# A hybrid decoder trunk on one core: recurrent projections first, attention columns later, and a second set of tiles for the recurrent group

## The chip, the cores and the metric

The kernel runs on one core of a Trainium2 chip. The core has five engines with their own instruction queues: TensorE (PE, matmuls, with its weight loads shown apart as PEld), VectorE (DVE), ScalarE (ACT), GpSimd (POOL) and SyncE (SP), which issues the DMAs here. The metric is device time of one execution in microseconds. Single executions are profiled; there is no number for a cost that is not read from such a profile.

## The reference, cut to what matters

Two layers, 256 tokens, width 2048, float32. Each layer has a mixer and a channel part:

```python
for l in range(2):
    mod = silu(c) @ w_ada[l] + b_ada[l]             # 6 vectors of 2048 ("ada")
    u = x * (1 + sc_m) + sh_m
    proj = u @ w_in[l]                              # 4896 columns
    q, k, v = proj[..., :1024], proj[..., 1024:1280], proj[..., 1280:1536]
    y_attn = sliding_window_attention(q, k, v, ...) # 16 heads of 64, 4 kv heads, window 128
    y_rwkv = rwkv7_group(proj[..., 1536:], ...)     # 16 heads of 64
    mix = concat([y_attn, y_rwkv]) @ w_out[l]
    x = layer_norm(alpha * x + gt_m * mix)
    u = x * (1 + sc_f) + sh_f
    gate, up = split(u @ w_gate_up[l])
    x = layer_norm(alpha * x + gt_f * ((silu(gate) * up) @ w_down[l]))
```

`rwkv7_group` shifts its columns by a token, splits them into r, k, v and three low-rank inputs, and runs a recurrence per head, one token after the other:

```python
S = S * w_t + (S @ a_t) b_t^T + v_t k_t^T           # S is 64 x 64 per head
o_t = S @ r_t
```

with a decay `w` and a gate `a` from low-rank products, then a group norm, a bonus term and a gate.

## The kernel before

**Precision.** Weights come in as float32 tiles of 512 KB (`raw`, L373), are cast on ACT to a rounded `hi` (L380) and the rest `lo = raw - hi` is made on DVE (L381, "the weight split"). Each product is then three matmuls, hi by hi, lo by hi, hi by lo: L402, L403, L405 where tokens are on the output's partitions (128x512 outputs), L414 to L416 in `tstream` where columns are (128x256 outputs). `raw` has 4 buffers, `hi` 3 and `lo` 2.

**Ada steps.** The modulation vectors are products of one row with `w_ada`: DVE sums a 512 KB tile `ast` times a scalar into `aacc` (L257), one step at a time, with two buffers. A pump in `steps()` and an `adv()` in the recurrence hand such steps out between other work; each is tied behind the latest weight split. SP issues all DMAs, weights, ada tiles and the mixer's own small ones, from one in-order queue.

**The mixer.** The recurrent part is done chunkwise: 4 chunks of 64 tokens, 8 pairs of heads in 4 groups of two pairs. For a group g the pieces are:

- D, `decays` (from L590): low-rank matmuls `zb` (L598) and `ab`, decay exponentials `e1` and `e2`, the gate `tha`, and `de`, three diagonal tiles per pair.
- R, `project` (from L576): the r and k columns by `tstream`.
- A, `prepare` (from L630): token shift, normalisation, the matrices `aa` (L684) and their masked copies `am` (L687), then `ax`, `at` (L702), `kb` (L710, the matmul with `de`) and `bnb` (L718).
- I, `invert` (from L723): the triangular inverse. The 16x16 diagonal blocks go out and in through DMA, POOL does 30 small steps (L729 to L735), DMA puts the result into `tinv` and back into `tm`, and two levels follow, each a DVE transpose `ytr` (L745), PE `m` (L749), DVE `yx` (L752), PE `m` (L756).
- C, `recur` (from L760): products with `tm`, then the chunk recurrence over ACT's state copies (L830).
- E, `close` (from L834): norm and gate.

Q0 to Q2, `project_qkv` (L869), are the attention columns in three blocks of 512, each with 96 matmuls and eight weight tiles; an ACT copy `stg` (L875) and a DMA write the block to `qkv` in HBM. X closes the pool of the recurrent tiles (`pa`) and opens that of attention (`pt`). Then a, b and c are the rotation (L884, reading `qkv` back), the weighting and the gathering for each of the four kv heads, and w and z the output projection (L995 on) over attention's and the recurrence's rows.

**What sets the order.** A string per layer, `ORDER` (L41), is the order in which the pieces are written. A scheduler then builds every engine's instruction stream ahead of the run, from that program order, the tiles' buffer counts and its own estimates; the streams are fixed and in order on each engine. A tile's buffer count says how many groups can hold it at the same time.

Of the kernel before, what the change touches and what calls it, by code (L numbers as in the profile page):

```python
# [10 lines left out]
F32 = mybir.dt.float32  # L11
# [8 lines left out]
P = 128  # L20
D = 2048
T = 256
# [16 lines left out]
DECAY = math.exp(-0.5)  # L39
NEG = -3.0e38  # L40
ORDER = (  # L41
    "D0 R0 A0 D1 I0 R1 C0 E0 Q1 A1 I1 D2 R2 A2 Q0 D3 C1 R3 E1 I2 A3 X Q2 a0 a1 b0 C2 a2 b1 c0 E2 a3 c1 I3 b2 b3 c2 c3 w0 C3 w1 w2 E3 z0 z1 z2 z3 w3",
    "D0 R0 A0 D1 R1 I0 C0 Q2 E0 A1 I1 D2 R2 A2 D3 Q1 C1 R3 E1 A3 I2 Q0 X a0 a1 b0 b1 c0 C2 I3 a2 b2 E2 a3 c1 b3 c2 c3 w0 C3 z0 w1 w2 E3 z1 z2 z3 w3",
)
PARTS = (4, 4, 2, 4, 2)
LAG = 2
# [21 lines left out]
def hybrid_trunk_kernel(  # L68
# [421 lines left out]
    def mixer(l, us, mixp, feeds):  # L490
# [7 lines left out]
        x0 = {}  # L498
        if rk:
            for i, s in ((0, 1), (0, 0), (1, 0)):  # L500
                x0[i, s] = pa.tile([P, T], F32, tag=("t_xr", "t_xk")[s], name="x0", bufs=2)
                shift_mix(l, x0[i, s], rk[i][s], 8 * s + i)
            turn[1] = 1

# [19 lines left out]
        if l > 0:  # L524
            v1t = pa.tile([P, NPAIR, 32], F32, tag="w2a2", name="v1t", bufs=1)
            dma(v1t, rwkv_v1[l - 1].rearrange("(q p) n -> p q n", p=P))
            hv = twd[64:96, :]
            b = bank()
            for p in range(NPAIR):
                PE.matmul(b[64:96, 0:T], lhsT=v1t[:, p, :], rhs=vx[:, p, :], start=(p == 0), stop=(p == NPAIR - 1))  # L530
            S.copy(hv, b[64:96, 0:T])
            for p2 in range(4):
                b = bank()
                v2t = pa.tile([P, T], F32, tag="w2a2", name="v2t", bufs=1)
                dma(v2t[64:96, :], rwkv_v2[l - 1, :, p2 * T:(p2 + 1) * T])
                for i in range(2):
                    p = 2 * p2 + i
                    PE.matmul(b[:, i * T:(i + 1) * T], lhsT=v2t[64:96, i * P:(i + 1) * P], rhs=hv, start=True, stop=True)
                for i in range(2):
                    p = 2 * p2 + i  # L540
                    gt = pa.tile([P, T], F32, tag="t_tha", name="gt", bufs=2)
                    S.activation(gt, b[:, i * T:(i + 1) * T], AF.Tanh, scale=0.5, bias=drv(l, "v0h", p))
                    vf = pa.tile([P, T], F32, tag="t_e2", name="vf", bufs=2)
                    dma(vf, vfirst[p])
                    V.tensor_sub(vf, vf, vx[:, p, :])
                    V.scalar_tensor_tensor(vf, gt, 1.0, vf, ALU.add, ALU.mult)
                    V.scalar_tensor_tensor(vx[:, p, :], vf, 0.5, vx[:, p, :], ALU.mult, ALU.add)
# [42 lines left out]
        def decays(g):  # L590
# [11 lines left out]
            for i in I2:  # L602
                s_, p = st[i], 2 * g + i
                lw = pa.tile([P, T], F32, tag="t_lw", name="lw", bufs=2)
                S.activation(lw, zb[:, i * T:(i + 1) * T], AF.Tanh, scale=0.5, bias=drv(l, "w0h", p))
                s_["tha"] = tha = pa.tile([P, T], F32, tag="t_tha", name="tha", bufs=2)
                S.activation(tha, ab[:, i * T:(i + 1) * T], AF.Tanh, scale=0.5, bias=drv(l, "a0h", p))
                V.tensor_scalar(lw, lw, -0.5 * DECAY, -0.5 * DECAY, ALU.mult, ALU.add)
                V.tensor_tensor_scan(lw, rmask, lw, 0.0, ALU.mult, ALU.add)
                s_["e1"] = e1 = pa.tile([P, NCH, CH + 1], F32, tag="e1", name="e1", bufs=2)  # L610
                V.memset(e1[:, :, 0:1], 1.0)
                S.activation(e1[:, :, 1:CH + 1], lw.rearrange("p (c s) -> p c s", s=CH), AF.Exp)
                s_["el"] = el = pb.tile([P, NCH, 1], F32, tag="el", name="el", bufs=4)
                G.tensor_copy(el, e1[:, :, CH:CH + 1])
                s_["de"] = de = pa.tile([P, NCH - 1, P], F32, tag="de", name="de", bufs=2)
                for cc in range(NCH - 1):
                    S.activation(de[:, cc, :], ident, AF.Copy, scale=e1[:, cc, CH:CH + 1])
                s_["e2"] = e2 = pa.tile([P, T], F32, tag="t_e2", name="e2", bufs=2)
                S.activation(e2, lw, AF.Exp, scale=-1.0)
            vt_ = bank("vt")  # L620
            for cc in range(NCH):
# [8 lines left out]
        def prepare(g, st, bk):  # L630

            nscr = dram.tile([4 * NCH, CH + 1, CH], F32, tag="nscr", name="nscr", bufs=3)
            for i in I2:
                s_, p = st[i], 2 * g + i
                for s, nm in ((1, "xk"), (0, "xr")):
                    if g == 0 and (i, s) in x0:
                        s_[nm] = x0[i, s]
                    else:
                        s_[nm] = pa.tile([P, T], F32, tag=f"t_{nm}", name=nm, bufs=2)
                        shift_mix(l, s_[nm], bk[i][:, s * T:(s + 1) * T], 8 * s + p)  # L640
            ssb = bank("ssb")
            for i in I2:
# [62 lines left out]
            for i in I2:  # L705
                s_ = st[i]
                bkc = s_["bkc"]
                kb = bank("kb")
                for cc in range(NCH - 1):
                    PE.matmul(kb[:, cc * P:(cc + 1) * P], lhsT=bkc[:, cc, :], rhs=s_["de"][:, cc, :], start=True, stop=True)  # L710
                s_["bkt"] = bkt = pb.tile([P, NCH - 1, P], F32, tag="bkt", name="bkt", bufs=4)
                S.copy(bkt.rearrange("p c s -> p (c s)"), kb[:, 0:(NCH - 1) * P])
            bnb = bank("bnb")
# [155 lines left out]
        def project_qkv(c0):  # L869
# [1 line left out]
            bk = acc_banks(1)  # L871
            stream(cols(w_in[l], c0, 512), 512, list(range(KT)), us, [(0, 512)], bk)
            for t in range(2):
                sg = (pt or pa).tile([P, 512], F32, tag="stg", name="stg", bufs=2)
                S.copy(sg, bk[t][0])  # L875
                dma(qkv[l, t, :, c0:c0 + 512], sg)

# [474 lines left out]
```

## Time and profile before

| | us |
|---|---|
| median of 3 runs | 2697.75 (2696.93 to 2700.12) |
| the profiled execution | 2698.87 |
| its span in the trace | 2697.1 |
| PE, DVE, ACT, POOL busy | 2507.4, 1843.0, 1189.2, 132.2 |
| prologue and the first projections of layer 0 | 0 to 178 |
| mixer, layer 0, projections; then inversion and attention | 178 to 423; 423 to 542 |
| mixer, layer 1, projections; then inversion and attention | 1518 to 1762; 1762 to 1845 |

The profiled execution's time and its span differ by 1.8 us, which lie around the first and last recorded instruction. Times in rows are from the span's start. A busy PE is not a PE at its peak; the granted clock beside it says how fast it ran.

### The profile page before, as it was taken

How to read it: one execution, taken by the hardware profiler on the slowest of the kernel's cores; microseconds unless marked ns; L12 is line 12 of the kernel's file. 1: busy time of each engine (PE TensorE's matmuls, PEld its weight loads, DVE VectorE, ACT ScalarE, POOL GpSimd, SP SyncE). 2: the span in 40 equal slices, each digit the busy share in tenths (PEclk: the TensorE clock that was granted, in tenths of full speed). 3: DMA queues.
4: the chain of work that ended last, by engine and by line, in shares of the span. 5: the costliest groups of instructions: out<-in, count | busy, mean ns of one | idle time of the engine just before them, and what ended most of it. 6: DMA issues, size and time to landing. Idle time of an engine off the chain costs nothing.

```text
span 2697.1 us, 41748 instructions
## 1 busy us (share of the span) xinstructions
PE 2507.4 (93%) x15325; PEld 2097.6 (78%) x15325; DVE 1843.0 (68%) x2469; ACT 1189.2 (44%) x2029; POOL 132.2 (5%) x355
## 2 busy tenths in 40 slices
PE   3789998797999999999999989989999999999997
PEld 3787886576878888888889877867788888888887
DVE  6867767979877777777788676565864545545456
ACT  2364452435444444444445544534444444344442
POOL 1002111000000000000000022110000000000000
PEclk9789997898999999999999999979999999999999
DMA  9968667598988888889878586424756655656654
GB/s 308 383 193 255 196 196 236 180 333 280 349 309 309 303 298 306 301 296 313 307 267 298 170 247 202 119 73 149 249 170 190 188 188 194 196 188 188 194 187 149
DMA packets 351999, 637.49 MB, mean 236 GB/s; under 512 B 75894, under 2 KB 142898, under 8 KB 350258
## 3 DMA queue, kind: packets, MB, share of 16 engines
q1 hardware_dynamic: 351794, 634.82, 71.4%
q8 instruction: 120, 1.97, 0.3%
q14 instruction: 85, 0.70, 0.1%
HBM read 622.08 MB, written 12.62 MB: 235 GB/s over the span
## 4 chain that ended last, share of the span: by engine, by line
PE 74%; DMA 12%; DVE 8%; issue 2%; POOL 2%; ACT 1%; SPq 1%; DVEq 0%; POOLq 0%; ACTq 0%
PE acc L403 19%; PE acc L405 19%; PE acc L402 19%; DMA ast<-in_w_ada_dram 7%; PE acc L416 3%; PE acc L415 3%; PE acc L414 3%; DVE lo L381 2%; DVE aacc L257 2%; DMA raw<-in_w_in_dram 1%; DMA raw<-in_w_gate_up_dram 1%; POOL tmp L733 1%; DMA raw<-in_w_out_dram 1%; PE aa L684 1%; PE mb L1225 1%
## 5 line engine op out<-in xcount | busy, mean ns | idle before, releaser
L380 ACT CAST hi<-raw 128x1024 fp32r<-128x1024 f32 (+2 forms) x728 | 758.3, 1044 | 1101.1 <-PE acc L405 811.6
L381 DVE TENSOR_TENSOR lo<-raw,hi 128x1024 fp32r<-128x1024 f32 (+2 forms) x728 | 880.6, 1212 | 519.4 <-PE acc L403 337.4
L403 PE MATMUL acc<-lo,u 128*128 128x512 f32 x1568 | 513.0, 394 | 9.2 <-DVE lo L381 9.2
L405 PE MATMUL acc<-hi,u 128*128 128x512 f32 x1568 | 506.1, 391 | 0.0
L257 DVE SCALAR_TENSOR_TENSOR aacc<-ast,cond,aacc 128x1024 f32<-128x1024 f32 x300 | 384.4, 1281 | 130.9 <-DMA ast<-in_w_ada_dram 129.6
L402 PE MATMUL acc<-hi,u 128*128 128x512 f32 x1568 | 458.0, 393 | 0.5 <-ACT u L360 0.5
L403 PEld LDWEIGHTS acc<-lo,u 128*128 128x128 f32 x1568 | 294.0, 189 | 74.2 <-DVE lo L381 13.4
L402 PEld LDWEIGHTS acc<-hi,u 128*128 128x128 f32 x1568 | 295.0, 189 | 62.2 <-ACT u L360 0.9
L405 PEld LDWEIGHTS acc<-hi,u 128*128 128x128 f32 x1568 | 295.2, 188 | 61.9 <-issue 0.7
L403 PE MATMUL acc<-lo,ht 128*128 128x512 f32 (+1 forms) x720 | 243.6, 377 | 2.7 <-DVE lo L381 2.6
L405 PE MATMUL acc<-hi,ht 128*128 128x512 f32 (+1 forms) x720 | 242.2, 375 | 0.0
L414 PE MATMUL acc<-u,hi 128*128 128x256 f32 x720 | 207.9, 295 | 13.1 <-ACT hi L380 13.1
L402 PE MATMUL acc<-hi,ht 128*128 128x512 f32 (+1 forms) x720 | 217.0, 376 | 0.0
L415 PE MATMUL acc<-u,hi 128*128 128x256 f32 x720 | 207.3, 295 | 0.0
L416 PE MATMUL acc<-u,lo 128*128 128x256 f32 x720 | 195.0, 297 | 3.5 <-DVE lo L381 3.5
L414 PEld LDWEIGHTS acc<-u,hi 128*128 128x128 f32 x720 | 144.3, 201 | 17.6 <-ACT hi L380 14.0
L403 PEld LDWEIGHTS acc<-lo,ht 128*128 128x128 f32 x720 | 135.0, 188 | 29.2 <-DVE lo L381 5.5
L405 PEld LDWEIGHTS acc<-hi,ht 128*128 128x128 f32 x720 | 135.6, 188 | 24.2
L402 PEld LDWEIGHTS acc<-hi,ht 128*128 128x128 f32 x720 | 134.8, 188 | 24.4
L415 PEld LDWEIGHTS acc<-u,hi 128*128 128x128 f32 x720 | 144.1, 200 | 3.6 <-issue 2.8
L416 PEld LDWEIGHTS acc<-u,lo 128*128 128x128 f32 x720 | 136.0, 201 | 7.7 <-DVE lo L381 5.1
L1067 POOL TENSOR_TENSOR brs<-brs,mhalf 128x1 f32<-128x1 f32 x8 | 6.5, 808 | 1705.3 <-DVE brs L1066 883.2
(349 smaller groups left out, 2887.8 us busy)
## 6 DMA issues: line engine op xcount, KB each, us to landing
ast<-in_w_ada_dram SPq DMA_DIRECT2D x368, 512.0 KB
raw<-in_w_gate_up_dram SPq DMA_DIRECT2D x704, 256.0 KB
raw<-in_w_down_dram SPq DMA_DIRECT2D x176, 512.0 KB
raw<-in_w_in_dram SPq DMA_DIRECT2D x82, 512.0 KB
raw<-in_w_out_dram SPq DMA_DIRECT2D x64, 512.0 KB
raw<-in_w_in_dram SPq DMA_DIRECT2D x120, 256.0 KB
ast<-in_w_ada_dram SPq DMA_DIRECT2D x32, 256.0 KB
lnw<-in_ln_w_dram SPq DMA_DIRECT2D x4, 1024.0 KB
```

The costliest lines, as they stand in the source:

```text
L257: ins = V.scalar_tensor_tensor(acc, t, cond[:, j:j + 1], acc, ALU.mult, ALU.add)
L380: S.copy(h, fl)
L381: ins = V.tensor_tensor(r, fl, h.bitcast(F32), ALU.subtract)
L402: PE.matmul(bt, lhsT=xh, rhs=hi[:, c0:c0 + w], start=st, stop=False)
L403: PE.matmul(bt, lhsT=xh, rhs=lo[:, c0:c0 + w], start=False, stop=False)
L405: PE.matmul(banks[t][q][:, 0:w], lhsT=xl, rhs=hi[:, c0:c0 + w], start=False, stop=sp_)
L414: PE.matmul(bt, lhsT=hi[:, c0:c0 + w], rhs=xh, start=st and opens, stop=False)
L415: PE.matmul(bt, lhsT=hi[:, c0:c0 + w], rhs=xl, start=False, stop=False)
L416: PE.matmul(bt, lhsT=lo[:, c0:c0 + w], rhs=xh, start=False, stop=sp_ and closes)
L684: PE.matmul(aas[h][:, cc * P:(cc + 1) * P], lhsT=bkc[hs, cc, :], rhs=ar[hs, cc, :], start=True, stop=True)
L733: G.tensor_tensor(tmp[:, 0:cm, 0:w], nb[:, s:s + 1, s + 1:].to_broadcast([P, cm, w]), tt[:, 0:cm, s:s + 1].to_broadcast([P, cm, w]), ALU.mult)
L1225: PE.transpose(b[:, i * T + t * P:i * T + (t + 1) * P], hh[t][:, (2 * k2 + i) * P:(2 * k2 + i + 1) * P], ident)
```

## The change

The diff. In both layers the string has the recurrent pieces first, Q1 behind A3, and Q0 and Q2 behind X; the tiles `xk`, `tha` (with `gt`), `e2` (with `vf`) and `e1` go from two to four buffers, `stg` from two to one, and the copies that make `de` move from `decays` to `prepare`.

```diff
 ORDER = (
-    "D0 R0 A0 D1 I0 R1 C0 E0 Q1 A1 I1 D2 R2 A2 Q0 D3 C1 R3 E1 I2 A3 X Q2 a0 a1 b0 C2 a2 b1 c0 E2 a3 c1 I3 b2 b3 c2 c3 w0 C3 w1 w2 E3 z0 z1 z2 z3 w3",
-    "D0 R0 A0 D1 R1 I0 C0 Q2 E0 A1 I1 D2 R2 A2 D3 Q1 C1 R3 E1 A3 I2 Q0 X a0 a1 b0 b1 c0 C2 I3 a2 b2 E2 a3 c1 b3 c2 c3 w0 C3 z0 w1 w2 E3 z1 z2 z3 w3",
+    "D0 R0 A0 D1 I0 R1 C0 A1 D2 I1 E0 R2 A2 D3 C1 I2 R3 E1 A3 Q1 C2 I3 X Q0 Q2 a0 a1 b0 E2 b1 c0 c1 a2 a3 b2 C3 b3 c2 E3 c3 w0 w1 w2 z0 z1 z2 z3 w3",
+    "D0 R0 A0 D1 R1 I0 C0 A1 D2 I1 E0 R2 A2 D3 C1 I2 R3 E1 A3 Q1 C2 I3 X Q0 Q2 a0 a1 b0 E2 b1 c0 c1 a2 a3 b2 C3 b3 c2 E3 c3 w0 w1 w2 z0 z1 z2 z3 w3",
 )
@@ mixer()
-                x0[i, s] = pa.tile([P, T], F32, tag=("t_xr", "t_xk")[s], name="x0", bufs=2)
+                x0[i, s] = pa.tile([P, T], F32, tag=("t_xr", "t_xk")[s], name="x0", bufs=(2, 4)[s])
...
-                    gt = pa.tile([P, T], F32, tag="t_tha", name="gt", bufs=2)
+                    gt = pa.tile([P, T], F32, tag="t_tha", name="gt", bufs=4)
...
-                    vf = pa.tile([P, T], F32, tag="t_e2", name="vf", bufs=2)
+                    vf = pa.tile([P, T], F32, tag="t_e2", name="vf", bufs=4)
@@ decays()
-                s_["tha"] = tha = pa.tile([P, T], F32, tag="t_tha", name="tha", bufs=2)
+                s_["tha"] = tha = pa.tile([P, T], F32, tag="t_tha", name="tha", bufs=4)
...
-                s_["e1"] = e1 = pa.tile([P, NCH, CH + 1], F32, tag="e1", name="e1", bufs=2)
+                s_["e1"] = e1 = pa.tile([P, NCH, CH + 1], F32, tag="e1", name="e1", bufs=4)
...
-                s_["de"] = de = pa.tile([P, NCH - 1, P], F32, tag="de", name="de", bufs=2)
-                for cc in range(NCH - 1):
-                    S.activation(de[:, cc, :], ident, AF.Copy, scale=e1[:, cc, CH:CH + 1])
-                s_["e2"] = e2 = pa.tile([P, T], F32, tag="t_e2", name="e2", bufs=2)
+                s_["e2"] = e2 = pa.tile([P, T], F32, tag="t_e2", name="e2", bufs=4)
@@ prepare()
-                        s_[nm] = pa.tile([P, T], F32, tag=f"t_{nm}", name=nm, bufs=2)
+                        s_[nm] = pa.tile([P, T], F32, tag=f"t_{nm}", name=nm, bufs=(2, 4)[s])
...
                 bkc = s_["bkc"]
+                de = pa.tile([P, NCH - 1, P], F32, tag="de", name="de", bufs=2)
+                for cc in range(NCH - 1):
+                    S.activation(de[:, cc, :], ident, AF.Copy, scale=s_["e1"][:, cc, CH:CH + 1])
                 kb = bank("kb")
                 for cc in range(NCH - 1):
-                    PE.matmul(kb[:, cc * P:(cc + 1) * P], lhsT=bkc[:, cc, :], rhs=s_["de"][:, cc, :], start=True, stop=True)
+                    PE.matmul(kb[:, cc * P:(cc + 1) * P], lhsT=bkc[:, cc, :], rhs=de[:, cc, :], start=True, stop=True)
@@ project_qkv()
-                sg = (pt or pa).tile([P, 512], F32, tag="stg", name="stg", bufs=2)
+                sg = (pt or pa).tile([P, 512], F32, tag="stg", name="stg", bufs=1)
```

In the streams below a row is a line, an operation, output and inputs, the output's shape and a count. Lines 617 to 704 of the changed kernel are three lower than the same code before.

PE in layer 0, from the last matmul of the attention columns (L405). Before:

```order
L405 MATMUL acc<-hi,u 128x512
L684 MATMUL aa<-ar,bkc 128x128 x8
L756 MATMUL m_4318<-tm,yx 64x64 x16
L695 MATMUL ax<-uv,am 64x64 x16
L702 MATMUL at<-ident,ar 64x128 x6
L769 MATMUL ta<-atl,tm 64x64 x11
L710 MATMUL kb<-de,bkc 128x128 x3
L769 MATMUL ta<-atl,tm 64x64
L710 MATMUL kb<-de,bkc 128x128 x3
L775 MATMUL tk<-uv,tm 64x64 x10
L718 MATMUL bnb<-xr,bones 128x256
```

Now:

```order
L405 MATMUL acc<-hi,u 128x512
L811 MATMUL ob<-state_1664,rh 64x128 x2
L814 MATMUL ob<-uv,am 64x64 x4
L749 MATMUL m_4543<-ytr,am 64x64 x16
L756 MATMUL m_4562<-tm,yx 64x64 x16
L906 MATMUL acc<-ident,qr 128x128 x6
L749 MATMUL m_4582<-ytr,am 64x64 x16
L906 MATMUL acc<-ident,qr 128x128 x4
L756 MATMUL m_4601<-tm,yx 64x64 x16
L906 MATMUL acc<-ident,qr 128x128 x2
L925 MATMUL acc<-qT 128x256 x4
```

Before, preparation of group 3 (`aa`, `ax`, `at`, `kb`, `bnb`) and the recurrence of group 2 (`ta`, `tk` with `tm` of the inversion before) stand behind the last projection matmul. Now they stand ahead of it, and what follows is the end of that recurrence (`ob`) and the inversion of group 3 (`m` with its `ytr` and `tm`), ahead of attention's transposes (L906).

DVE in layer 0, around the transpose `ytr` of the last inversion before the change:

```order
L894 TENSOR_TENSOR ra<-qk,cosk 128x640
L895 TENSOR_TENSOR rb<-qk,sink__147 128x640
L852 TENSOR_SCALAR vr<-vr 128x8
L898 TENSOR_TENSOR qr<-ra,rb 128x5x32
L899 TENSOR_TENSOR qr<-ra,rb 128x5x32
L898 TENSOR_TENSOR qr<-ra,rb 128x5x32
L899 TENSOR_TENSOR qr<-ra,rb 128x5x32
L257 SCALAR_TENSOR_TENSOR aacc<-ast,cond,aacc 128x1024
L854 TENSOR_TENSOR sq<-os__4848,vr 128x512
L257 SCALAR_TENSOR_TENSOR aacc<-ast,cond,aacc 128x1024
L745 STREAM_TRANSPOSE ytr<-tm 128x512
L894 TENSOR_TENSOR ra<-qk,cosk 128x640
```

The same transpose, that of group 3's inversion, in the changed kernel (`bv` ends group 3's preparation, L381 are weight splits, L894 is the first rotation):

```order
L720 TENSOR_TENSOR bv<-bnb,vx 128x256
L381 TENSOR_TENSOR lo<-raw,hi 128x1024
L745 STREAM_TRANSPOSE ytr<-tm 128x512
L255 TENSOR_SCALAR aacc<-ast,cond 128x1024
L257 SCALAR_TENSOR_TENSOR aacc<-ast,cond,aacc 128x1024
L381 TENSOR_TENSOR lo<-raw,hi 128x1024
L284 SCALAR_TENSOR_TENSOR mods_135<-asum,par_131 128x8
L257 SCALAR_TENSOR_TENSOR aacc<-ast,cond,aacc 128x1024
L381 TENSOR_TENSOR lo<-raw,hi 128x1024
L894 TENSOR_TENSOR ra<-qk,cosk 128x640
```

Before, the transpose stands behind the first rotation (`ra` to `qr`) and ada steps (L257), and ahead of the second rotation. Now it stands one weight split behind the preparation's `bv`, ahead of two weight splits, ada steps and the first rotation.

DVE in layer 1, at the transpose of group 2's inversion. Before:

```order
L381 TENSOR_TENSOR lo<-raw,hi 128x1024
L745 STREAM_TRANSPOSE ytr<-tm 128x512
L798 TENSOR_TENSOR mt<-mr,mt 128x256
L800 TENSOR_TENSOR rh<-mr,ar 128x192
L798 TENSOR_TENSOR mt<-mr,mt 128x256
L800 TENSOR_TENSOR rh<-mr,ar 128x192
L381 TENSOR_TENSOR lo<-raw,hi 128x1024 x4
L455 SCALAR_TENSOR_TENSOR xk<-acc,par_132,xk 128x255 x2
```

Now:

```order
L455 SCALAR_TENSOR_TENSOR xr<-acc,par_132,xr 128x255
L745 STREAM_TRANSPOSE ytr<-tm 128x512
L662 SCALAR_TENSOR_TENSOR ar<-xk,der_134,e_15817 128x4x64
L675 TENSOR_TENSOR ar<-xr,e_15817 128x4x64
L798 TENSOR_TENSOR mt<-mr,mt 128x256
L800 TENSOR_TENSOR rh<-mr,ar 128x192
L662 SCALAR_TENSOR_TENSOR ar<-xk,der_134,e_15830 128x4x64
L675 TENSOR_TENSOR ar<-xr,e_15830 128x4x64
L381 TENSOR_TENSOR lo<-raw,hi 128x1024 x7
L752 TENSOR_TENSOR yx<-m_16056,mmask 128x512
```

The transpose `ytr` and six instructions of preparation and recurrence stand ahead of seven weight splits; before, four recurrence instructions and then four splits stood behind it.

## The prediction

> **What bounds the kernel now.** I read the page first, then the stretches of the two mixers engine by engine, then single instructions at the seams. The page says where there is room:
>
> ```profile
> span 2697.1 us, 41748 instructions
> PE 2507.4 (93%) x15325; PEld 2097.6 (78%) x15325; DVE 1843.0 (68%) x2469; ACT 1189.2 (44%) x2029; POOL 132.2 (5%) x355
> PEclk9789997898999999999999999979999999999999
> ```
>
> TensorE (PE) is busy 93% of the span, and the granted clock dips in slices 6 to 8 (337 to 539 us) and 28 (1821 to 1888 us): the ends of the two mixers. The change edits only the mixers, so I cut these into stretches. Columns: window, length, busy us of PE, weight load, VectorE (DVE), ScalarE (ACT), GpSimd (POOL), granted clock, DMA share, GB/s.
>
> ```profile
> 178.00:423.00 245.00, 234.87 (x2244) 201.81 (x2243) 179.78 (x275) 124.82 (x249) 40.98 (x103) 0.96 0.72 221
> 423.00:464.00 41.00, 32.30 (x313) 24.74 (x312) 26.29 (x39) 13.07 (x41) 11.64 (x33) 0.72 0.77 216
> 464.00:542.00 78.00, 56.96 (x558) 44.38 (x557) 71.44 (x192) 31.75 (x120) 2.22 (x3) 0.78 0.61 183
> 1518.00:1762.00 244.00, 230.98 (x2195) 195.86 (x2193) 165.39 (x257) 122.03 (x257) 46.32 (x103) 0.97 0.63 190
> 1762.00:1791.00 29.00, 18.65 (x293) 14.90 (x292) 12.84 (x27) 9.88 (x24) 9.55 (x33) 0.85 0.45 108
> 1791.00:1845.00 54.00, 48.48 (x511) 36.80 (x510) 39.08 (x157) 25.69 (x98) 1.34 (x3) 0.83 0.04 11
> ```
>
> Rows one and four are the projections: PE has 10 us idle in 245 and 13 us in 244, so PE sets the pace. Behind them come *bare* stretches without projection matmuls. The second and fifth are inversions, chains over POOL, DMA and DVE. The third is attention in layer 0, with DVE busy 71.4 of 78 us: there DVE sets the pace. PE idles 8.7, 21.0, 10.4 and 5.5 us in the bare rows. The seams (columns: start, length, engine, line, operation, tiles; in brackets the idle time before and its releaser):
>
> ```profile
> 178.07 0.48 PE L598 MATMUL zb<-twd,w2a 64*128 64x256 f32 x1
> 421.62 0.39 PE L405 MATMUL acc<-hi,u 128*128 128x512 f32 x1
> 426.56 0.68 DVE L687 TENSOR_TENSOR am<-aa,amask 128x512 f32<-128x512 f32 x1
> 464.20 0.71 DVE L745 STREAM_TRANSPOSE ytr<-tm 128x512 f32<-128x512 f32 x1
> 530.61 0.50 PE L402 MATMUL acc<-hi,yl 128*128 128x512 f32 x1
> 542.42 2.35 DVE L381 TENSOR_TENSOR lo<-raw,hi 128x1024 fp32r<-128x1024 f32 x2
> 1761.50 0.40 PE L403 MATMUL acc<-lo,u 128*128 128x512 f32 x1
> 1761.73 0.40 PE L405 MATMUL acc<-hi,u 128*128 128x512 f32 x1
> 1763.25 1.29 DVE L687 TENSOR_TENSOR am<-aa,amask 128x512 f32<-128x512 f32 x2
> 1790.83 0.71 DVE L745 STREAM_TRANSPOSE ytr<-tm 128x512 f32<-128x512 f32 x1 [1.05 <-DMA tm<-tinv]
> 1845.19 0.50 PE L402 MATMUL acc<-hi,yl 128*128 128x512 f32 x1
> ```
>
> Layer 0: the last query/key/value matmul starts at 421.6, the last inversion runs from its mask (am, done at 427.2) to its transpose (ytr) at 464.2, 37.0 us, the first output-projection matmul at 530.6, and DVE is through with attention at 542.4, where the projection's third weight split starts. Layer 1: 1761.7, 1790.8, 1845.2. Starts of neighbouring matmuls lie 0.23 us apart. Behind both seams PE is saturated until the layer's end, so what the change is worth is how far 542.4 and 1845.2 move.
>
> **The double tiles and `de`.** By the order, decays D(n+1)'s first matmul (zb) stands right behind preparation A(n)'s last (bnb) before the change, and still does or is at most a few projection matmuls later. The second set of tiles therefore moves the decays hardly at all: 0. The `de` copies are the same three ACT instructions per pair, on an engine busy 125 of 245 us: 0, between -1 and +1 for both together. What acts is the new string: recurrences earlier, and A3's tail with C2 under query/key/value projections where they stood behind the last of these.
>
> **Layer 0, the projections.** The moved work costs PE time in a full stretch. A window that holds such a pair (A2's tail with C1, and decays D3), and in it the projection's matmuls alone:
>
> ```profile
> 350.00:381.00 31.00, 31.00 (x378) 27.58 (x378) 12.09 (x19) 18.10 (x46) 9.24 (x33) 1.00 0.43 109
> 350.00:381.00 31.00, 16.58 (x118) 14.57 (x118) 0.00 (x0) 0.00 (x0) 1.00 0.43 109
> ```
>
> 31.0 - 16.6 = 14.4 us, less about 2 for D3 (my estimate): the moved pair costs 12 to 13 us, 12.5 taken. The last projection matmul goes from 421.6 to 434.1, if no inversion is late. Whether one is depends on its length:
>
> ```profile
> 290.15 0.28 PE L415 MATMUL acc<-u,hi 128*128 128x256 f32 x1
> 290.27 0.28 PE L416 MATMUL acc<-u,lo 128*128 128x256 f32 x1
> 290.03 1.29 DVE L687 TENSOR_TENSOR am<-aa,amask 128x512 f32<-128x512 f32 x2 [0.65 <-PE aa L684]
> 315.88 0.70 DVE L745 STREAM_TRANSPOSE ytr<-tm 128x512 f32<-128x512 f32 x1
> 217.44 1.28 DVE L687 TENSOR_TENSOR am<-aa,amask 128x512 f32<-128x512 f32 x2
> 254.05 0.70 DVE L745 STREAM_TRANSPOSE ytr<-tm 128x512 f32<-128x512 f32 x1
> 251.34 1.28 DVE L257 SCALAR_TENSOR_TENSOR aacc<-ast,cond,aacc 128x1024 f32<-128x1024 f32 x1 [6.98 <-DMA ast<-in_w_ada_dram]
> 227.50:246.00 18.50, 18.50 (x96) 14.47 (x95) 14.12 (x17) 10.28 (x21) 15.79 (x30) 1.00 0.62 225
> 297.50:309.20 11.70, 11.70 (x108) 8.75 (x106) 4.66 (x9) 8.73 (x23) 8.98 (x32) 1.00 0.40 131
> ```
>
> From the mask's end to ytr it is 24.6 us (291.3 to 315.9) or 35.3 (218.7 to 254.1). POOL's thirty small steps take 9.0 us beside a quiet DVE (4.7 busy of 11.7) and 15.8 beside a busy one (14.1 of 18.5). The 7 us wait for `ast` sits at the end of the slow chain, since its loads stand on SyncE's queue behind the inversion's own, and ytr stands behind that step on DVE.
>
> In the new order PE has, between group 1's `aa` and its first inversion matmul, 72 receptance/key matmuls 0.12 us apart (8.6), such a pair (C0 with A1's tail, 12.5) and D2 (2): 23 us. A chain of 25 to 37 leaves PE waiting 2 to 14 us, and I take 7, the side of the quick one. The second inversion has more cover: 0 to 6, taken 2. The last projection matmul is then at 434.1 + 9 = 443 (435 to 453).
>
> Group 3's mask is some 28 us ahead of that (75 matmuls of 0.23, and 11 of the moved 12.5), at 415. With a chain of 25 to 37, taken 31 since DVE there still splits weights, ytr is at 446 instead of 464.2: **18 us won**, 439 to 452.
>
> **Layer 0, attention.** DVE's queue between ytr and the third output split now holds more, because ytr moved ahead of it: by the order 33 ada steps for 26, 188 other instructions for 166.
>
> ```profile
> 464.00:542.00 78.00, 31.98 (x26) 0.78 0.61 183
> L257 DVE SCALAR_TENSOR_TENSOR aacc<-ast,cond,aacc 128x1024 f32<-128x1024 f32 x34 | 43.7, 1285 | 15.7 <-DMA ast<-in_w_ada_dram 15.3
> L894 DVE TENSOR_TENSOR ra<-qk,cosk 128x640 f32<-128x640 f32 x4 | 3.3, 824 | 0.2 <-DMA qk<-qkv 0.2
> L895 DVE TENSOR_TENSOR rb<-qk,sink__147 128x640 f32<-128x640 f32 x4 | 3.3, 816 | 0.0
> L898 DVE TENSOR_TENSOR qr<-ra,rb 128x160 f32<-128x160 f32 x8 | 2.6, 320 | 0.1
> ```
>
> Line one is the ada part (L257) of the attention stretch, the others are groups of 423 to 540. The added work is 7 ada steps at 1.29 (9.0), two rotations at 0.82 + 0.82 + 4 x 0.32 = 2.9 (5.8), and two weight splits of 2.35 together (row at 542.42): 17.2, some 17.5 with E2's small ones. So 71.4 + 17.5 = 88.9 us of DVE work. Before, 6.6 us of 78 were waits; I take 7.5, between 0 and 15 (C2's and E2's matmuls are no longer in this stretch, but I3's now stand at its start). 446 + 96.4 = 542.4, against 542.4: **0**. By that time some ten fewer output matmuls are done, since E2's and attention's feeds for them come later: 10 x 0.23 = 2.3. **Layer 0: +3**, from -8 (439, no added wait) to +16 (452, 104 us).
>
> **Layer 1.** Its slow spot before:
>
> ```profile
> 1659.67 1.29 DVE L257 SCALAR_TENSOR_TENSOR aacc<-ast,cond,aacc 128x1024 f32<-128x1024 f32 x1 [6.92 <-DMA ast<-in_w_ada_dram]
> 1662.14 0.79 PE L403 MATMUL acc<-lo,u 128*128 128x512 f32 x1 [4.82 <-DVE lo L381]
> PE mb L277 <- DVE aacc L257: 7.1, 1, 7.1
> 1791.00:1845.00 54.00, 0.00 (x0) 0.83 0.04 11
> ```
>
> There a late ada step held a weight split and so PE, 4.8 and 7.1 us; these waits go or change place (between 0 and -12, -6 taken). New is that group 2's ytr stands on DVE ahead of seven weight splits: PE has 46 projection matmuls whose weights are split and a pair of 12.5 until it needs them, 23 us against a chain of 25 to 37: wait 2 to 14, 8 taken, and 2 for group 1. With the moved 12.5 the last matmul goes from 1761.7 to 1778 (1768 to 1788). Group 3's mask lies 16 us ahead of it (34 matmuls and 8 of the moved work), at 1762; with the 26.3 of before (1764.54 to 1790.83) ytr comes at 1788 to 1789, where it was at 1790.8. The stretch behind it took 54.4 and no ada step lies in it. C2 has left it, but attention's rotations and E2 have not, so PE's part shrinks little: between 52 (its 48.5 busy us and few waits) and 64 (the inversion stretch's 10.4 us of idle on top), and I take 58, the middle. 1789 + 58 = 1847 against 1845.2; **+3** with the single staging tile's small waits in it, from -7 (ytr at 1783 and 55 us) to +12 (1793 and 64).
>
> **Sum.** +3 and +3 on the profiled 2698.87 gives 2705; that execution is 1.1 above the median of 2697.75, so **2704**.
>
> The Trainium skill, "SBUF — State Buffer", section "Who interferes with whom", says that a DVE instruction with two SBUF inputs contends with a GpSimd instruction that reads SBUF. The rows 15.79 beside 14.12 and 8.98 beside 4.66 agree with it. By that rule alone every inversion laid under weight splits runs at the slow pace, and the sum would be 2704 + 2 x 5 = 2714, an estimate.
>
> **The rivals.** 0.2% of 2698 is 5.4 us, about what a measurement of this kernel can tell from no change.
> (a) *Forecast, slower by some us*, 0.39: PE pays 12.5 us per layer in full stretches, and what it frees is eaten by DVE's longer attention queue. For: DVE busy 71.4 of 78. Against: PE idles 21 us there. Range of its own 2699 to 2716.
> (b) *No change*, 0.25: the decays stay where they are, and what ytr wins in each layer the stretch behind it loses, to a few us: 2698. For: both sums above end within 3 us of zero. Against: they have bounds of 19 and 24 us between them, and nothing makes the two sides equal.
> (c) *Faster*, 0.30: the inversions keep the fast pace (24.6) because DVE has fewer late ada steps beside them. Then PE waits nowhere in the projections (ytr at 439 and 1783): -7 and -6 against the profiled run, 2698.9 - 13 - 1.1 = 2685, itself 2680 to 2692. For: 4.8 and 7.1 us that layer 1 loses now. Against: both slow chains lie where DVE splits weights.
> (d) *The single staging tile*, 0.06: its second copy (L875) waits on ACT for the first write, which on SyncE's queue stands behind the last inversion's `tinv` and `tm` loads. C2's state copies and a weight cast stand behind it on ACT. If the write is held for the whole POOL part (9 to 16 us), one such hold in each layer adds 5 to 8 beside what PE still has to do: 2704 + 11 = 2715. It decides once the write's issue is more than about 5 us late.
>
> The likeliest is (a), 2704. From (c)'s lower part to the upper bounds of (a) and (d), 2682 to 2724 leaves about 2 in 10 out. Slower: four fifths of (a) and (d), 0.37; same: (b) and the rest of (a), 0.33; faster: (c), 0.30.
>
> **What would show it.** Layer 0's last inversion transpose at 446 and the third output split at 542 or later, with DVE over 85 us busy between. The last projection matmuls near 443 and 1778. Waits of PE for DVE at m (L749) or at a weight split, 2 to 14 us, at the inversions of group 1 in layer 0 and group 2 in layer 1. Wrong: those waits absent and the output projection beginning before 526 or 1840, which is (c); or a gap on ACT ahead of the second staging copy over 5 us, which is (d).

## The result and the profile after

The changed kernel took 2710.22 us (median of 5 runs, 2704.71 to 2714.87) against 2697.75 (5 runs); the ratio is 1.0035, with a 95% interval of 1.0018 to 1.0052. Run once more beside the experiments it took 2708.05 (8 runs), ratio 1.0031 (1.0018 to 1.0044). It is slower by 10 to 12 us between medians; the forecast was 2704, 6 us slower.

The page of the changed kernel. The profiled execution took 2704.71 us, the quickest of its five.

```profile
span 2703.0 us, 41745 instructions
PE 2502.6 (93%) x15325; PEld 2094.4 (77%) x15325; DVE 1841.0 (68%) x2469; ACT 1188.5 (44%) x2029; POOL 133.2 (5%) x355
PEclk9899998799999999999999998979999999999999
```

All engines are busy for about the same time as before. The windows are cut at the same events as before the change (columns as in the prediction): projections, last inversion, attention, for each layer.

```profile
174.00:419.00 245.00, 228.87 (x2363) 196.09 (x2363) 181.56 (x278) 120.38 (x246) 42.53 (x103) 0.97 0.70 212
419.00:444.00 25.00, 21.54 (x147) 17.06 (x145) 10.14 (x13) 7.46 (x19) 10.86 (x30) 0.93 0.72 215
444.00:548.00 104.00, 65.86 (x609) 50.94 (x609) 88.24 (x220) 44.15 (x163) 7.32 (x6) 0.74 0.67 205
1517.00:1762.00 245.00, 233.88 (x2355) 199.43 (x2354) 166.83 (x261) 120.30 (x255) 41.78 (x107) 0.97 0.63 184
1762.00:1779.00 17.00, 12.55 (x117) 9.58 (x115) 4.75 (x6) 8.04 (x17) 8.19 (x27) 0.95 0.40 115
1779.00:1855.00 76.00, 61.59 (x547) 46.17 (x548) 47.91 (x178) 31.90 (x109) 4.46 (x6) 0.72 0.13 39
```

The seams of the changed kernel, from its timeline:

```profile
174.15 0.48 PE L598 MATMUL zb<-twd,w2a 64*128 64x256 f32 x1
443.14 0.71 DVE L745 STREAM_TRANSPOSE ytr<-tm 128x512 f32<-128x512 f32 x1 [5.07 <-DMA tm<-tinv]
443.76 0.39 PE L405 MATMUL acc<-hi,u 128*128 128x512 f32 x1
541.48 0.47 PE L402 MATMUL acc<-hi,yl 128*128 128x512 f32 x1
548.04 1.23 DVE L381 TENSOR_TENSOR lo<-raw,hi 128x1024 fp32r<-128x1024 f32 x1 [1.82 <-PE acc L403]
1517.25 0.48 PE L598 MATMUL zb<-twd,w2a 64*128 64x256 f32 x1
1772.39 0.39 PE L405 MATMUL acc<-hi,u 128*128 128x512 f32 x1
1778.81 0.71 DVE L745 STREAM_TRANSPOSE ytr<-tm 128x512 f32<-128x512 f32 x1 [4.93 <-DMA tm<-tinv]
1854.76 0.50 PE L402 MATMUL acc<-hi,yl 128*128 128x512 f32 x1
```

In layer 0 the last inversion's transpose comes 21 us earlier than before (443.1 for 464.2), the last projection matmul 22 us later, and the first output-projection matmul 11 us later (541.5 for 530.6); this execution entered the layer 3.9 us earlier, so counted from the layer's first decay matmul it is 14.8. In layer 1 the transpose comes 12 us earlier (1778.8 for 1790.8) and the first output matmul 9.6 us later (1854.8 for 1845.2). In both layers the inversion is won and the start of the output projection is lost.

What the late start is worth differs. These are windows of the output projections, of layer 0 and of layer 1, in the kernel before:

```profile
560.00:600.00 40.00, 35.24 (x148) 26.95 (x147) 29.91 (x36) 13.35 (x14) 0.00 (x0) 1.00 0.98 365
1855.00:1900.00 45.00, 43.59 (x192) 35.12 (x191) 27.12 (x38) 20.23 (x23) 0.14 (x1) 1.00 0.76 270
```

and that of layer 0 in the changed kernel:

```profile
560.00:600.00 40.00, 38.56 (x166) 30.26 (x165) 32.49 (x37) 14.75 (x15) 0.00 (x0) 1.00 0.97 371
```

In layer 0 the projection caught up: its last matmul started at 635.1 before and at 635.0 now, 3.9 us late instead of 14.8 when counted from the layer's start. From its first matmul to its last it took 104.5 us before and 93.5 now. The DMA engines are as busy in the one as in the other (0.98 and 0.97), so their share does not tell the two apart. PE's waits do (who waited for what, us in total, times, longest). Before, from 530.6 to 636, PE was idle for 9.0 us, with these among its waits:

```profile
PE acc L402 <- DVE yl L460: 2.7, 1, 2.7
PE acc L402 <- ACT yl L459: 1.4, 1, 1.4
```

Here `yl` is a row of attention or recurrence, rounded for the projection. In the changed kernel, from 541.5 to 636, PE was idle for 2.1 us, and its waits are for weights alone:

```profile
PE acc L403 <- DVE lo L381: 1.0, 4, 0.3
PE acc L402 <- ACT hi L380: 0.9, 1, 0.9
```

The other part of the 11 us is PE's own pace: in the first 29 us of the projection the granted clock was 0.94 before and 1.00 after. The later profiles agree: this projection takes 101.9 to 104.6 us with the old string in layer 0, with 7.7 to 9.5 us of idle time and `yl` among the waits, and 93.5 to 97.4 with the new string, with 2.1 to 4.1 us idle and no wait for `yl`. The new string closes the recurrence (C3, E3) ahead of the projection, which fits; which of its pieces frees the rows was not taken apart. In layer 1 PE was idle for 1.8 us of this projection before, and 3 of the 11 us were made up (95.0 and 92.2 us).

### The profile page after: what moved, and what is told of

It is laid out like the page before. It is cut to its first block, busy times and chain, and to the rows that moved or that the text cites. A ratio compares the mean times of both kernels' runs of the same rounds, so it can differ in the third digit from the quotient of the medians.

```text
span 2703.0 us, 41745 instructions
## 1 busy us (share of the span) xinstructions
PE 2502.6 (93%) x15325; PEld 2094.4 (77%) x15325; DVE 1841.0 (68%) x2469; ACT 1188.5 (44%) x2029; POOL 133.2 (5%) x355
## 4 chain that ended last, share of the span: by engine, by line
PE 60%; DMA 4%; DVE 4%; POOL 1%; ACT 1%; issue 1%; SPq 0%; DVEq 0%; POOLq 0%; ACTq 0%
PE acc L403 17%; PE acc L405 17%; PE acc L402 17%; DVE lo L381 1%; PE acc L414 1%; PE acc L415 1%; PE acc L416 1%; POOL tmp L733 1%; DMA raw<-in_w_gate_up_dram 1%; PE mb L1225 1%; DVE aacc L257 1%; DMA raw<-in_w_out_dram 1%; DMA nscr<-am 1%; POOL ttl L735 1%; DMA nb<-nscr 0%
## 5 line engine op out<-in xcount | busy, mean ns | idle before, releaser
L381 DVE TENSOR_TENSOR lo<-raw,hi 128x1024 fp32r<-128x1024 f32 (+2 forms) x728 | 879.9, 1211 | 513.7 <-PE acc L403 350.4
L405 PE MATMUL acc<-hi,u 128*128 128x512 f32 x1568 | 507.7, 392 | 0.0
L257 DVE SCALAR_TENSOR_TENSOR aacc<-ast,cond,aacc 128x1024 f32<-128x1024 f32 x300 | 383.8, 1279 | 128.2 <-DMA ast<-in_w_ada_dram 127.2
L405 PEld LDWEIGHTS acc<-hi,u 128*128 128x128 f32 x1568 | 296.0, 189 | 62.4 <-DVE u L361 0.3
L403 PE MATMUL acc<-lo,ht 128*128 128x512 f32 (+1 forms) x720 | 243.5, 377 | 2.2 <-DVE lo L381 2.2
L405 PE MATMUL acc<-hi,ht 128*128 128x512 f32 (+1 forms) x720 | 242.2, 375 | 0.0
L414 PEld LDWEIGHTS acc<-u,hi 128*128 128x128 f32 x720 | 143.5, 200 | 15.8 <-ACT hi L380 12.5
L405 PEld LDWEIGHTS acc<-hi,ht 128*128 128x128 f32 x720 | 135.6, 188 | 24.3
```

The source lines that it names most:

```text
L257: ins = V.scalar_tensor_tensor(acc, t, cond[:, j:j + 1], acc, ALU.mult, ALU.add)
L381: ins = V.tensor_tensor(r, fl, h.bitcast(F32), ALU.subtract)
L403: PE.matmul(bt, lhsT=xh, rhs=lo[:, c0:c0 + w], start=False, stop=False)
L405: PE.matmul(banks[t][q][:, 0:w], lhsT=xl, rhs=hi[:, c0:c0 + w], start=False, stop=sp_)
L414: PE.matmul(bt, lhsT=hi[:, c0:c0 + w], rhs=xh, start=st and opens, stop=False)
```

## The experiments

The execution of one kernel differs from the next by up to 10 us (2704.71 to 2714.87 above), and in the profiles of kernels with the same layer 0 the first decay matmul of layer 1 lay anywhere from 1510 to 1520 us. So seams are counted here from the first decay matmul (zb, L598) of their own layer, and medians decide. "Old" and "new" are the two order strings.

**1. The tiles without the strings.** `ORDER` of before in the changed kernel; all buffer counts and the place of `de` as changed.

```diff
-    "D0 R0 A0 D1 I0 R1 C0 A1 D2 I1 E0 ...",   # new, both layers
+    "D0 R0 A0 D1 I0 R1 C0 E0 Q1 A1 I1 ...",   # old, both layers
```

> The changed tiles (four buffers for xk, tha, e2 and e1, one for stg, the de copies in prepare) with the old order string in both layers. My theory, that the string alone acts and the second set of tiles hardly moves the decays: no change, 2695 to 2701 beside a before of 2698. Rival, that the wider or narrower tile sets carry the loss (the single staging tile holding ACT): 2703 or more even with the old string.

Measured: 2692.82 (11 runs; before 2698.51 in this set), ratio 0.9982 (0.9972 to 0.9992): 5.7 us faster than before. Neither expectation has it. In the order of PE's stream the decays of group n+1 still stand behind `bnb` of group n with these tiles. In time they do move in layer 1: `zb` of groups 1, 2 and 3 starts 52.6, 115.1 and 173.4 us behind the layer's first one, for 59.4, 126.1 and 183.3 before, and group 3's mask (am) 225.6 for 241.3; in layer 0 the `zb` move by no more than 2 us. Whether this is the gain, and which of the tile edits makes it, was not taken apart further than in experiment 11.

**2 and 3. One layer at a time.**

```diff
 ORDER = (
-    new layer 0, new layer 1
+    new layer 0, old layer 1      # experiment 2
+    old layer 0, new layer 1      # experiment 3
 )
```

> The change in layer 0 alone; layer 1 keeps its old string, the tiles are the changed ones. The two traces put the change's loss into layer 1: the channel part of layer 0 starts 1.0 us earlier than before, and the end is 5.9 later. Theory: no change here, 2694 to 2702. Rival, that layer 0 has a share of the loss that this one profiled execution does not show (executions of the change spread over 10 us): 2703 to 2708.

> The change in layer 1 alone; layer 0 keeps its old string. Theory: attention there is a chain of some 83 us that hangs on the last projection matmul (1761.7 to 1845.2 before, 1772.4 to 1854.8 in the change), and that matmul comes 11 us later: slower by 7 to 12, 2704 to 2710. Rival, that the loss is in layer 0: 2696 to 2701.

Measured: 2695.97 with the new string in layer 0 (11 runs, ratio 0.9986, 0.9976 to 0.9996) and 2709.45 with it in layer 1 (6 runs, 1.0038, 1.0024 to 1.0051). Against the same tiles with old strings (2692.8) layer 0's string costs 3 us, little more than can be told, and layer 1's costs 17. The loss is layer 1's. Its seams, first with the new string in layer 0 alone, then in layer 1 alone:

```profile
1523.33 0.48 PE L598 MATMUL zb<-twd,w2a 64*128 64x256 f32 x1
1766.27 0.40 PE L405 MATMUL acc<-hi,u 128*128 128x512 f32 x1
1840.40 0.50 PE L402 MATMUL acc<-hi,yl 128*128 128x512 f32 x1
```

```profile
1516.83 0.48 PE L598 MATMUL zb<-twd,w2a 64*128 64x256 f32 x1
1777.76 0.39 PE L405 MATMUL acc<-hi,u 128*128 128x512 f32 x1
1856.88 0.50 PE L402 MATMUL acc<-hi,yl 128*128 128x512 f32 x1
```

From the decays to the last projection matmul layer 1 takes 242.9 us with the old string and 260.9 with the new one; from there to the output projection 74.1 and 79.1. These two profiles lie far apart: with the changed tiles and the whole old or new string (experiments 1 to 3, the change and experiment 9) it is 242.9 and 247.9 us against 253.6 to 260.9, and the stretch behind it 74.1 and 77.7 against 79.1 to 85.8. So the last projection matmul came 6 to 18 us later, and attention behind it did not become shorter. PE's busy time up to that matmul is 232.7 us of 243 in experiment 2 and 246.1 of 261 in experiment 3: the work moved ahead of it costs 13 us of PE, and PE idles 5 us more.

**4. The staging tile.**

```diff
-                sg = (pt or pa).tile([P, 512], F32, tag="stg", name="stg", bufs=1)
+                sg = (pt or pa).tile([P, 512], F32, tag="stg", name="stg", bufs=2 if pt else 1)
```

> The change with two staging tiles again for Q0 and Q2 (the pool of attention has room for them), one for Q1. Rival (d) of the prediction, the single staging tile: in the change's trace the staging copies of ACT wait 5.6 and 3.6 us for their predecessor's write, and PE 8.5 us for the last of them at the inversion in layer 0; by it the kernel is 4 to 12 us faster than the change, 2698 to 2706. By the theory that DVE's queue (layer 0) and the attention chain (layer 1) set the ends, the stall of PE is cover only, and it stays at 2708 to 2712.

Measured: 2717.36 (6 runs), ratio 1.0065 (1.0051 to 1.0079): not faster. The wait was real. In the changed kernel, layer 0, ACT's staging copies and PE:

```profile
443.68 0.59 ACT L875 COPY stg<-acc 128x512 f32<-128x512 f32 x1 [5.61 <-DMA qkv<-stg]
448.53 0.59 ACT L875 COPY stg<-acc 128x512 f32<-128x512 f32 x1
454.80 0.59 ACT L875 COPY stg<-acc 128x512 f32<-128x512 f32 x1 [3.59 <-DMA qkv<-stg]
PE m L756 <- ACT stg L875: 8.5, 1, 8.5
```

PE waits 8.5 us for the last one, yet a second tile for Q0 and Q2 wins nothing with the new string. In its profile, which is its quickest execution (2708.17), the first output matmul of layer 0 lies 367.3 us from the decays, as in the change, and in layer 1 the last projection matmul, 255 us from the decays in the change, came at 259. The edit does not take all of rival (d) away: in layer 1 the first staged block was copied at 1778.5 and its write issued at 1785.7, still behind the inversion's loads on SyncE's queue. With experiment 8, which has two staging tiles too, it shows that the loss does not need the single tile.

**5. The moved pieces put back.** In experiments 5 to 7, 10 and 11 layer 0 has its old string. New string in layer 1 as far as `A3 Q1`, but C2 and I3 behind the projections.

```diff
-  ... A3 Q1 C2 I3 X Q0 Q2 a0 a1 b0 E2 b1 c0 c1 a2 a3 b2 C3 b3 c2 E3 c3 w0 w1 w2 z0 ...
+  ... A3 Q1 X Q0 Q2 a0 a1 b0 b1 c0 C2 I3 a2 b2 E2 a3 c1 b3 c2 c3 w0 C3 z0 w1 w2 E3 ...
```

> Changed tiles, old string in layer 0; layer 1 has the new string as far as A3 Q1, then Q0 and Q2, and C2, I3 and the rest in the old order behind them: of the new string only the move of C2 and of A3's tail ahead of the last projection matmuls is undone. Theory (attention is a chain of fixed length, 77 to 83 us, that hangs on the last projection matmul, and the recurrence work put ahead of that matmul delays it): the matmul comes 10 to 12 us earlier than with the whole new string, and the time is 2692 to 2699, near the 2692.8 of the old string with the same tiles. Rival (the order of attention's and the recurrence's pieces behind it, or the projections being late as a block, costs the time): 2703 or more.

Measured: 2696.97 (12 runs), ratio 1.0002 (0.9989 to 1.0015). 12.5 of the 16.6 us come back. The last projection matmul lies 249.6 us behind the decays (260.9 with the whole new string).

**6. Only the order behind the projections put back.**

```diff
-  ... A3 Q1 C2 I3 X Q0 Q2 a0 a1 b0 E2 b1 c0 c1 a2 a3 b2 C3 b3 c2 E3 c3 w0 w1 w2 z0 ...
+  ... A3 Q1 C2 I3 X Q0 Q2 a0 a1 b0 b1 c0 a2 b2 E2 a3 c1 b3 c2 c3 w0 C3 z0 w1 w2 E3 ...
```

> Changed tiles, old string in layer 0; layer 1 has the new string up to Q2, with C2 and I3 ahead of Q0, and behind it the old order of the attention and closing pieces. Theory of the late last projection matmul: still slow, 2704 to 2711, as layer 1's whole new string (2709.5). Rival, that the new order of the pieces behind Q2 makes attention long: 2692 to 2699.

Measured: 2702.11 (12 runs), ratio 1.002 (1.0008 to 1.0031), between the two expectations. In its profile the stretch is no shorter than in experiment 3 (last projection matmul at 261.6, first output matmul at 341.7 for 340.1), but the median is 7 us lower. So the order behind Q2 may carry some of the loss; the profile does not show where, and this stays open.

**7. All projections still earlier.** In layer 1 Q1, Q2 and Q0 stand ahead of A3, then the old order.

```diff
-  ... R3 E1 A3 Q1 C2 I3 X Q0 Q2 a0 a1 b0 E2 b1 c0 ...
+  ... R3 E1 Q1 Q2 Q0 A3 X a0 a1 b0 b1 c0 C2 I3 a2 ...
```

> Changed tiles, old string in layer 0; layer 1 with all receptance/key projections first, then Q1 Q2 Q0 ahead of A3, then the old order. The last projection matmul is a further 8 to 10 us of PE work earlier than with C2 and I3 undone. Theory: the time follows it down, 2684 to 2693. Rival, that the recurrence (A3, I3, C3, E3 one behind the other) is then the longer chain: 2694 to 2706.

Measured: 2701.23 (12 runs), ratio 1.0013 (1.0003 to 1.0023). The rival is right: the last projection matmul comes at 243.5 us, as early as with the old string, but the last inversion's transpose only at 277.4 (258.8 in experiment 1), and the output projection at 329.8. The chain that ended last runs there over that inversion's mask and POOL steps: the recurrence is then the longer chain. The old string stands between two losses.

**8. The strings without the tiles.**

```diff
-    bufs=4 / (2, 4)[s] / stg bufs=1 / de in prepare()
+    bufs=2 / 2         / stg bufs=2 / de in decays()
```

> The new strings in both layers with the old tiles (two buffers each, two staging tiles, de in decays). Prediction's step that the second set of tiles hardly moves the decays: within 6 us of the change, 2704 to 2716. Rival, that the new string lives on the second set, and the decays stand behind the preparation without it: 2720 or more.

Measured: 2706.59 (12 runs), ratio 1.0038 (1.0022 to 1.0055): as the change. The new strings do not live on the second set of tiles, and with them the tiles gain nothing that shows (2706.6 without, 2708 to 2710 with).

**9. The change again.** No edit.

> The change once more, beside the others of this set: 2705 to 2713. Its second profile tells whether the lateness sits in layer 1: from the first decay matmul of layer 1 to the first output-projection matmul 335 to 341 us (326.7 before, 337.5 in the change's first profile).

Measured: 2708.05, and in this profile 339.4 us from layer 1's first decay matmul to its first output matmul: with 337.5 and 326.7 (before) the lateness in layer 1 is seen twice.

**10. One piece ahead, in the old string.**

```diff
-  ... A3 I2 Q0 X a0 a1 b0 b1 c0 C2 I3 a2 ...
+  ... A3 I2 C2 Q0 X a0 a1 b0 b1 c0 I3 a2 ...
```

> Changed tiles, old strings, and in layer 1 one piece moved: C2, the recurrence of group 2, written ahead of Q0 instead of behind c0. Theory of the late last projection matmul: C2's PE work of 6 to 8 us and its waits go ahead of that matmul, it comes 6 to 12 us later than in the old string with the same tiles, and the time rises from 2692.8 to 2697 to 2704. Rival, that only the whole block of late projections (all receptance/key first) or the attention order costs: 2690 to 2696.

Measured: 2697.0 (12 runs), ratio 0.9989 (0.9976 to 1.0001), 4.2 us above the same tiles with the old string. The last projection matmul comes at 250.8 us (242.9 to 247.9 in experiments 1, 2 and 11, which have this layer's old string and the new tiles), the first output matmul at 332.9 (317.1 to 325.6). C2 alone, put ahead of the last projection block, delays the output projection in this profile; a part is made up behind it. The medians alone do not settle it: the interval overlaps that of experiment 1.

**11. The best of both.** Old strings, changed tiles, the staging edit of experiment 4.

> Changed tiles with the old strings (2692.8), and two staging tiles for the projections in attention's pool, as in the run that gave the change a second one. If the single staging tile costs anything with the old string (its second copy there came 6 us after the last projection matmul in layer 1, 0.4 us before): 2687 to 2692. If the tile is cover only: 2690 to 2696.

Measured: 2690.03 (5 runs, 2688.56 to 2694.12), ratio 0.9963 (0.9948 to 0.9978). This is faster than the kernel before by 7.6 us and than the change by 18. Against experiment 1 the intervals overlap, so the second staging tile's own share is not shown.

**12. Fewer ada steps in layer 0.** Experiment 2 with one ada step for each recurrence step.

```diff
-AR = (3, 7)
+AR = (1, 7)
```

> Changed tiles, new string in layer 0, old in layer 1 (2696.0), and in layer 0 one ada step for each recurrence step instead of three: by the order 20 instead of 33 ada steps between the last inversion's transpose and the third output split, the others later. The prediction's step that DVE's queue sets the length of attention in layer 0: the stretch from the last projection matmul to the first output matmul falls from 97.5 by 10 to 17 us. What the end does with it tells the second point: if the transfers set the pace of the output projection behind it (DMA busy 95 to 98% there), the gain is given back and the time stays at 2692 to 2700; if DVE alone did, 2680 to 2690.

Measured: 2749.18 (4 runs), ratio 1.0181 (1.0162 to 1.02). Both expectations of the time are wrong; the one of the stretch is met at its upper edge. From the last projection matmul to the first output matmul of layer 0, for this kernel:

```profile
452.23 0.39 PE L405 MATMUL acc<-hi,u 128*128 128x512 f32 x1
532.54 0.50 PE L402 MATMUL acc<-hi,yl 128*128 128x512 f32 x1
452.00:532.50 80.50, 20.36 (x16) 0.75 0.50 157
```

and for the changed kernel, the ada steps (L257) of the same stretch, in the same columns:

```profile
444.00:542.00 98.00, 38.40 (x30) 0.72 0.67 206
```

14 ada steps fewer are 18.0 us less on DVE, and the stretch is 17.4 us shorter (80.3 for 97.7): what these steps take on DVE comes off the stretch, one for one. Their loads are gone from it too (DMA share 0.50 for 0.67), and the run does not part the two.

The second question of the expectation, whether transfers set the pace behind the stretch, has its answer in the trace. The output projection starts 354.9 us from the decays and its last matmul 449.8; in experiment 2 these are 367.6 and 462.8. The start is 12.7 us earlier and the end 13.0: the gain was kept through the whole projection, with the DMA engines 94% busy or more from 560 on. Then the debt comes due. PE's wait ahead of the channel part of layer 0, in the waits of this kernel:

```profile
PE mb L277 <- DVE aacc L257: 34.3, 1, 34.3
```

The channel part needs the sums that were put off. An ada step in the attention stretch is a payment, not a loss: put off, it cost more where it was due. Of the 49 us between this profile and that of experiment 2, 26 lie in layer 0; another 21 lie behind the first decay matmul of layer 1, where the strings are the same. There the last projection matmul comes at 261.6 us, not 242.9: DVE is busy for 11 us more up to it, and PE is idle for 23 us instead of 10, on `ytr` and weight splits among others. Why DVE has more to do there was not looked into.

## Why the prediction was right, and where it was not

**The sign and the size.** Forecast +6, measured +12 and +10 by the two medians. The parts did not come as forecast: tiles -5.7 for 0, layer 0 +3 for +3, layer 1 +17 for +3. Layer 1's string lies outside its bounds of -7 to +12. That the whole stayed within the range is luck: the tiles won back a part that nobody had forecast. The parts, each between medians a few us uncertain, sum to +14, a little more than the change itself.

**The double tiles: a term put at nothing.** The prediction read from the order that the decays stay behind `bnb`, which is so, and took from it that they do not move. In layer 1 they came 7 to 11 us earlier (experiment 1), and the kernel with the tiles alone was 5.7 us faster. That the one is the cause of the other is not shown.

**Layer 0, the projections: right.** From the layer's first decay matmul the last projection matmul was put at 265 us (443 in the time of before) and came at 269.6; the last transpose was put at 268 and came at 269.0.

**Layer 0, attention: right in mechanism, short in size, and repaid.** DVE's 88.9 us of work were 88.2 in the window from 444 to 548, and its waits were 15.8, not 7.5; 8.0 of them were for `ast` tiles (DVE aacc L257 <- DMA ast). So the third output split came 373.9 us from the decays where 364.3 was forecast. The forecast took this seam's shift, with 2.3 us for later output matmuls, as the layer's loss. In fact the output projection made up most of it. The step that failed is "Behind both seams PE is saturated until the layer's end": PE was idle for 9.0 us of the projection behind the seam before, and for 2.1 after, as its waits for `yl` went. It was not that transfers bound it, since in experiment 12 an earlier start was kept to the end. Two errors met, and +3 came out.

**Layer 1: the term that was mis-sized.** The price of the moved work, 12.5 us of PE, was about right (13 in experiments 2 and 3). The last projection matmul was put at 1778 (259.5 from the decays) and came at 255.1 in the first profile, 253.6 and 260.9 in others; ytr was put at 1789 and came at 1778.8. The stretch behind it was given 58 us between 52 and 64, and measured 76.0. So ytr came 10 us early and the stretch was 18 us longer. The prediction took it as a sum of PE's work and idle times, from which C2 could be taken away, "with the single staging tile's small waits in it". These waits were not small. It is a chain over SyncE's queue, ACT's staging, the DMAs to HBM and back, DVE's rotation and four rounds of weights. The chain of waits of the changed kernel has it (start, length, what):

```profile
1772.25 0.60 SPq L738
1772.90 2.15 DMA tinv<-ttl
...
1776.49 2.83 DMA qkv<-stg
1779.39 0.59 ACT stg L875
1780.01 3.56 DMA qkv<-stg
...
1787.29 0.59 ACT stg L875
1788.27 2.94 DMA qk<-qkv
1791.34 0.83 DVE ra L894
...
1854.83 0.43 PE acc L402
```

The first of the last four staged blocks was copied from 1769.0 to 1769.6, but its write was issued at 1776.5, 6.9 us later, behind the DMAs of the last inversion (tinv, tm) on SyncE's queue. Each of the other three copies then waited some 3 us on ACT for the write before it. The last copy starts 14.9 us behind the last projection matmul. Before, it was 0.4 us:

```profile
1761.47 1.28 ACT L875 COPY stg<-acc 128x512 f32<-128x512 f32 x2 [3.37 <-PE acc L405]
```

This is what rival (d) said. With one staging tile and the old string (experiments 1 and 2) the last copy came 6.0 and 5.9 us behind that matmul, with the new string 14.9 to 15.2; with two staging tiles and the new string (experiments 4 and 8) 8.2 and 6.3, and the stretch was 76.6 and 76.8 us where one tile had 79.1 to 85.8. In both of these runs the last projection matmul came late, 259.0 and 260.4 us from the decays, and neither was faster than the change. So the staging is a part of the long stretch, and its share of the loss is not shown.

From the last projection matmul it takes 74 to 86 us in layer 1 in the profiles of all these kernels. Two windows show that C2's leaving did not shorten it. The 83 us behind the last projection matmul of layer 1, before and after the change:

```profile
1762.00:1845.00 83.00, 67.13 (x803) 51.70 (x802) 51.92 (x183) 35.57 (x121) 10.89 (x35) 0.84 0.18 45
```

```profile
1772.00:1855.00 83.00, 64.15 (x593) 47.99 (x590) 49.33 (x179) 35.86 (x119) 4.68 (x7) 0.73 0.16 47
```

210 PE instructions fewer, and PE is busy for 3 us less. The granted clock went from 0.84 to 0.73. The same groups of matmuls, before and then after (mean ns of one stands behind the busy time):

```profile
L977 PE MATMUL acc<-pts,vt 128*64 128x128 f32 x30 | 5.1, 304 | 0.3 <-DVE pts L971 0.3
L981 PE MATMUL acc<-pts,vt 128*64 128x128 f32 x28 | 3.7, 273 | 0.0
```

```profile
L977 PE MATMUL acc<-pts,vt 128*64 128x128 f32 x30 | 7.6, 385 | 1.3 <-ACT pts L969 0.8 <-DVE pts L971 0.5
L981 PE MATMUL acc<-pts,vt 128*64 128x128 f32 x28 | 5.2, 337 | 0.0
```

The Trainium skill, "TensorE: Matmul & The Clock Gate", section "Part 1: The HAM clock gate (the "warmup" mystery)", says that the array's default is the throttled clock and that activity releases it. The rows agree: with fewer matmuls in the stretch the clock was lower and each took longer. That the clock alone keeps the chain at its length is not shown: in experiment 3 the stretch was 79.1 us at a granted clock of 0.78, and the longer waits on DVE and DMA belong to it too.

**The waits in the projections: partly.** Of the forecast waits of 2 to 14 us, layer 0's group 1 had 1.0 us at ytr (5.5 in group 0) and a weight split 3.7 beside group 2's inversion; layer 1's group 2 had none. POOL's part took 13.1 us in layer 0's last inversion (422.5 to 435.6) and 11.2 in layer 1's (1761.0 to 1772.2), between the quick 9.0 and the slow 15.8 of before, so neither pace can be taken for a new place. Layer 1's last inversion took 23.7 us from mask to transpose, as rival (c) wanted it, and its gain did not follow. The late ada step that held PE 7.1 us in layer 1 is gone in the change (0.3 us), and this too was not kept.

**Rivals.** (b) was right that the decays keep their place in the order, but in time they moved in layer 1. (c) had layer 1's inversion right and the end wrong. (d) had six chances in a hundred, and its mechanism is there: both of its signs, a gap over 5 us on ACT ahead of a staging copy (5.61 in layer 0) and a write issued more than 5 us late (6.9 in layer 1), are met, and PE waited 8.5 us in layer 0. Experiments 4 and 8 show that the loss does not need the single tile; they leave open what SyncE's queue costs, since no run takes the staged writes out from behind the inversion's loads.

## What to carry to other kernels

A bare stretch behind a saturated one is shortened by moving work out of it only if that work is on the stretch's own chain, and it can grow by what the move puts in the way of that chain. Here, in layer 1, the chain hung on the last projection matmul, the staged writes and the last inversion. What was put ahead of that matmul made it 6 to 18 us later, and the inversion's loads, now issued at the same time as the staged writes, held these. So list, for the new order, what an in-order queue is asked for in the same few microseconds.

And ask at each seam which waits of the bottleneck lie behind it: a start 15 us late was mostly made up in layer 0, where the work behind it had 9 us of idle time to lose, and a start 11 us late was mostly kept in layer 1, where it had 1.8. A busy share of the DMA engines does not answer this; the waits do.

## What had not been expected

- The changed tiles with the old strings are faster than before, 0.9982, and with two staging tiles 0.9963, though the decays keep their place in the order.
- PE busy time is no measure of work in a thin stretch: 593 instructions kept PE busy for 64.15 us at a clock of 0.73, 803 for 67.13 at 0.84.
- Putting 14 ada steps off shortened one stretch by 17.4 us and stalled PE by 34.3 us at the place where their sums were due.
